# Hybrid trunk kernel: latent norm sums, row maxima and the start of the attention rewritten

## The chip, the core and the metric

The kernel runs on one core of one Trainium2 chip. The metric is the device time of one execution in microseconds (us). The engines are TensorE (PE in the rows; PEld is its weight load), VectorE (DVE), ScalarE (ACT), GpSimd (POOL) and SyncE (SP), which issues every DMA of this kernel in one queue.

## The reference

Two layers work on 768 tokens (256 context, 512 latent) of width 1024. Each layer projects the tokens to three head groups (a state space mixer, latent attention, retention), joins them, projects back and normalizes. Layer 1 returns latent tokens alone. What the change touches is the latent attention:

```python
def rms_norm(x, g):
    xf = x.astype(jnp.float32)
    return (xf * lax.rsqrt(jnp.mean(xf * xf, -1, keepdims=True) + RMS_EPS)).astype(x.dtype) * g

def project(cq, ckv, kr, rope):            # inside mla_mixer
    q = (rms_norm(cq, q_norm) @ w_uq).reshape(b, n, 8, 64 + 32)
    kv = (rms_norm(ckv, kv_norm) @ w_ukv).reshape(b, n, 8, 64 + 64)
    ...                                    # split into nope/rope parts, rope on latent tokens

def mla_attend(q_nope, q_rope, k_nope, k_rope, v):
    s = (jnp.einsum('bqhd,bkhd->bhqk', q_nope, k_nope)
         + jnp.einsum('bqhr,bkr->bhqk', q_rope, k_rope)).astype(jnp.float32) * MLA_SCALE
    pr = jax.nn.softmax(s, axis=-1).astype(v.dtype)
    return jnp.einsum('bhqk,bkhd->bqhd', pr, v)
```

cq is 384 wide, ckv 256 wide. There are 8 heads. Context queries see context keys, latent queries see all.

## The kernel before

All activations lie transposed: a tile is 128 channels by 768 tokens, and the 768 tokens are 6 chunks of 128. A product of full precision is made of three fp32r matmuls (`mm3`): each operand is split into a rounded high part and the remainder (`split`: one ScalarE cast, one VectorE subtraction), and the low-times-low product is left out.

A layer runs in stages: the input projection with the state space mixer, the retention (`ret`), the gate tiles (`zstage`, products `pj`), the preparation of the attention (`mla_prep`), the norm of the mixer (`ztail`), the attention (`mla`), and the output projection in two halves: `out_s` (products `po` with `sh`, `sl`; eight tiles) and `out_m` (`po` with `mr`, `mh`). A scheduler reorders the instructions of each engine by priority and dependence, so the written order sets priorities and not positions: work written later fills places where earlier work is not ready. Each engine then runs its own list strictly in order.

`mla_prep` normalizes ckv and cq (`normed`, L877). For each tile of 128 channels it loads `nx`, makes the scaled high and low parts `nh` and `nl`, squares `nx` on ScalarE and sums the squares over channels with fp32 matmuls against ones into the rows of one PSUM tile (`pn`, L892). `rowcols` (L659) copies those rows to SBUF and turns them with four fp32 matmuls into columns (`pcol`), one column for each chunk; `rstd_all` takes the inverse square root of the columns on VectorE (`rya`) and spreads it back with fp32 matmuls against the identity (`prs`). Then come the key product `pkn`, the value product `pvv` and the query product `pq`, with weights `pwh`, `pwl`.

The attention holds two buffers of operands, one for even and one for odd heads (`mla`, L966). `mla_max` (L985) loads a head's queries, keys and values, splits them, forms the score of the high parts for each chunk of 128 queries (`pmx`), takes the negated row maxima on VectorE (`nm`), splits these into two bf16 tiles (`nmh`, `nml`) and turns each chunk's column into a row with two bf16 matmuls against an identity (`pnm`). ScalarE copies the row to row 96 of the query operand `bqh`, so that the score product (`psc`, 97 rows) subtracts the maximum. `mla_head` (L1022) makes the scores, two exponentials (`pe`, `peh`), a subtraction (`pel`) and the value product (`ppv`). `mla_max` of head h+1 is written ahead of `mla_head` of head h.

`load_mix` (L407) loads the four retention outputs `m` (tile `mraw`) and splits them to `mr`, which `out_m` uses; it is written ahead of the attention.

Of the kernel before, what the change touches and what calls it, by code (L numbers as in the profile page):

```python
# [8 lines left out]

F32 = mybir.dt.float32  # L10
F32R = mybir.dt.float32r
BF16 = mybir.dt.bfloat16
I32 = mybir.dt.int32
AF = mybir.ActivationFunctionType
ALU = mybir.AluOpType
# [16 lines left out]
XP = 776  # L32
XC = 772

(C_ID, C_MF, C_MB, C_R1, C_R2, C_OD, C_PF, C_PB, C_SD, C_SM, C_S2, C_PE, C_PR, NCONST) = (
    0, 128, 256, 384, 512, 640, 768, 896, 1024, 1152, 1280, 1283, 1285, 1287)

(P_CW, P_CB, P_D, P_NW, P_QN, P_KN, P_BA, P_LG, P_LB, P_RF, P_RB, P_DT, P_AL, P_RR, NPC) = (
    0, 60, 72, 80, 88, 91, 93, 117, 125, 133, 135, 137, 169, 201, 209)

RROW = {NCTX: 0, 0: 64}

Z_T, X_T, B_T, Q_T, KV_T, G_T, RQ_T, RK_T, RG_T, RV_T, M_T, NWIN = (
    0, 8, 16, 20, 23, 25, 29, 31, 33, 37, 41, 42)
# [23 lines left out]
def const_pack():  # L68
    p = np.arange(128)
    j, i = p[:, None], p[None, :]  # L70
    c = np.zeros((128, NCONST), np.float32)
    c[:, C_ID:C_ID + 128] = j == i
    c[:, C_MF:C_MF + 128] = j <= i
    c[:, C_MB:C_MB + 128] = j >= i
    c[:, C_R1:C_R1 + 128] = np.maximum(i - j, 0)
    c[:, C_R2:C_R2 + 128] = np.maximum(j - i, 0)
    c[:, C_OD:C_OD + 128] = (1.0 + (j == i)) * 0.125
    c[:, C_PF:C_PF + 128] = i + 1 + 0 * j
    c[:, C_PB:C_PB + 128] = 128 - i + 0 * j
    first = (p % 32 == 0).astype(np.float32)  # L80
    c[:, C_SD:C_SD + 128] = 1.0 / DM
    c[:, C_SM:C_SM + 128] = 1.0 / (DM // 2)
    c[:, C_S2] = first
    c[:, C_S2 + 1] = p % 32 == 1
    c[:, C_S2 + 2] = 0
    c[:, C_PE] = 127 - p
    c[:, C_PE + 1] = p
    c[:, C_PR] = first * (p >= 64)
    c[:, C_PR + 1] = first * (p < 64)
    return c  # L90


class Trunk:
# [146 lines left out]
    def consts(self):  # L240
        nc = self.nc
        c = self.cp.tile([128, 8, 2], F32, name="cT")
        self.load(c, self.A["cT"])
        self.pc = [self.cp.tile([128, NPC], F32, name=f"pc{l}") for l in range(DEPTH)]
        self.load(self.pc[0], self.A["pc"][0])
        self.K = self.cp.tile([128, NCONST], F32, name="K")
        self.load(self.K, self.A["cpack"])
        k = lambda a, n=128: self.K[:, a:a + n]
        self.ident, self.mf, self.mb = k(C_ID), k(C_MF), k(C_MB)
        self.selD, self.selM, self.sel2 = k(C_SD), k(C_SM), k(C_S2, 2)  # L250
        self.ones = self.cp.tile([128, 128], F32, name="ones")
        nc.vector.memset(self.ones, 1.0)
        self.rsb = self.cp.tile([128, T], F32, name="rsb")
        self.identb = self.cp.tile([128, 128], BF16, name="identb")
        nc.vector.tensor_copy(self.identb, self.ident)
        self.mod = [self.cp.tile([128, 24, 2], F32, name=f"mod{l}") for l in range(DEPTH)]
        self.sil = self.cp.tile([128, 8, 32], F32, name="sil")
        nc.vector.memset(self.sil, 0.0)
        v = self.cp.tile([128, 8, 2], F32, name="cv")
        self.ts(v, c, 0.5, ALU.mult)  # L260
        th = self.cp.tile([128, 8, 2], F32, name="cth")
        self.act(th, v, AF.Tanh)
        self.stt(self.sil[:, :, 0:2], th, 1.0, v, ALU.add, ALU.mult)
# [65 lines left out]
    def layer(self, l):  # L329
# [44 lines left out]
        with self.lpool(f"mixr{l}") as MR:  # L374
            self.mr = [[MR.tile([128, T], F32R, name=f"mr{i}{t}") for t in range(4)] for i in range(2)]
            self.m3 = MR.tile([128, T], F32, name="m3")
            self.load_mix(range(4, 8), *self.mr)
            with self.lpool(f"mla{l}") as P, self.ppool(f"mlaps{l}") as self.px:
                self.mla(P)
                for t in range(8):  # L380
                    self.out_s(t)
                with self.tc.high_priority():
                    self.mla_last(P)
            self.mixpool.close()
            if l + 1 < DEPTH:
                self.open_h(l + 1)
            with self.rpool(f"mixm{l}") as R, self.lpool(f"outm{l}") as P, self.ppool(f"outmp{l}") as self.px:
                self.out_m(R, P)
# [267 lines left out]
    def blocks(self):  # L656
        return ([(0, NCTX)] if self.ctx else []) + [(NCTX, T)]

    def rowcols(self, P, prow, bl):  # L659

        rows = P.tile([128, 512], F32, tag="rrow", name="rrow", bufs=1)
        pc = self.ps("prs", "pcol", 1)
        nr = 64 * len(bl)
        if nr == 128:
            self.nc.gpsimd.memset(rows[64:128, NCTX:512], 0.0)
        for a, b in bl[::-1]:
            r = slice(RROW[a], RROW[a] + 64)
            self.copy(rows[r, 0:b - a], prow[r, 0:b - a])
        for c in range(4):
            cs = slice(c * 128, c * 128 + 128)  # L670
            if nr == 128 and c < 2:
                self.mm(pc[:, c:c + 3:2], rows[:, cs], self.K[:, C_PR:C_PR + 2])
            else:
                self.mm(pc[:, c + 2:c + 3], rows[:nr, cs], self.K[:nr, C_PR + 1:C_PR + 2])
        return pc

    def rstd_all(self, P, pc, bl, scale, eps, out):

        c0 = bl[0][0] // 128
# [190 lines left out]
    def mla_prep(self, P):  # L870
# [7 lines left out]
        def normed(src, nt, col, width, full):  # L878
            a0 = 0 if full else NCTX
            hi, lw = [], []  # L880
            bl = ([(0, NCTX)] if full else []) + [(NCTX, T)]
            prow = self.ps("prow", "pn", 1)
            for t in range(nt):
                x = P.tile([128, T], F32, tag="nx", name="nx", bufs=3)
                self.load(x[:, a0:], src[t][:, a0:])
                h = P.tile([128, T], F32R, tag="nhl", name="nh", bufs=6)
                w = P.tile([128, T], F32R, tag="nhl", name="nl", bufs=6)
                self.split(h[:, a0:], w[:, a0:], x[:, a0:], pc[:, col + t:col + t + 1])
                self.act(x[:, a0:], x[:, a0:], AF.Square)
                for a, b in bl:  # L890
                    g = RROW[a] + 32 * (t % 2)
                    self.mm(prow[g:g + 32, 0:b - a], self.ones[:, 0:32], x[:, a:b],  # L892
                            start=t < 2, stop=t >= nt - 2, skip_group_check=True)
                hi.append(h)
                lw.append(w)
            rb = P.tile([128, T], F32, tag="nrb", name="nrb", bufs=1)
            y = self.rstd_all(P, self.rowcols(P, prow, bl), bl, 1.0 / width, RMS_EPS, rb)
            return hi, lw, rb, y

        kh, kl, krb, ky = normed(D["ckv"], 2, P_KN, 256, True)  # L900
# [64 lines left out]

    def mla(self, P):  # L966
        nc, ctx = self.nc, self.ctx
        self.B = []
        for i in range(2):
            b = dict(  # L970
                qh=P.tile([97, T], F32R, name=f"bqh{i}"), ql=P.tile([97, T], F32R, name=f"bql{i}"),
                kh=P.tile([97, T], F32R, name=f"bkh{i}"), kl=P.tile([97, T], F32R, name=f"bkl{i}"),
                vh=P.tile([128, NCH, 128], F32R, name=f"bvh{i}"), vl=P.tile([128, NCH, 64], F32R, name=f"bvl{i}"))
            nc.vector.memset(b["ql"][96:97, :].bitcast(F32), 0.0)
            nc.vector.memset(b["kh"][96:97, :].bitcast(F32), 1.0)
            nc.vector.memset(b["kl"][96:97, :].bitcast(F32), 0.0)
            nc.vector.memset(b["vh"][:, :, 64:128].bitcast(F32), 1.0)
            self.B.append(b)
        self.mla_max(P, 0)
        for h in range(8):  # L980
            if h + 1 < 8:
                self.mla_max(P, h + 1)
            self.mla_head(P, h)

    def mla_max(self, P, h):  # L985

        nc, D, ctx, lo = self.nc, self.D, self.ctx, self.lo
        b, (p, s) = self.B[h % 2], divmod(h, 2)
# [8 lines left out]
        self.split(b["qh"][0:96, lo:], b["ql"][0:96, lo:], q[:, lo:])  # L997
        self.split(b["kh"][0:96, :], b["kl"][0:96, :], k)
        self.split(b["vh"][:, :, 0:64], b["vl"], self.vr[:, :, s * 64:(s + 1) * 64])
        qt = [0, 1, 2, 3, 4, 5] if ctx else [2, 3, 4, 5]  # L1000
        nq = len(qt)
        nm = P.tile([128, 6], F32, tag="nm", name="nm", bufs=2)
        for i, c in enumerate(qt):
            p1 = self.px.tile([128, 1024], F32, tag="pmx", name="pmx", bufs=1)
            n = NCTX if c < 2 else T
            for a in range(0, n, 512):
                self.mm(p1[:, a:min(a + 512, n)], b["qh"][0:96, c * 128:(c + 1) * 128], b["kh"][0:96, a:min(a + 512, n)])
            nc.vector.tensor_reduce(nm[:, i:i + 1], p1[:, 0:n], axis=AX.X, op=ALU.max, negate=True)  # L1008
        nmh = P.tile([128, 6], BF16, tag="nmh", name="nmh", bufs=2)
        nml = P.tile([128, 6], BF16, tag="nml", name="nml", bufs=2)  # L1010
        nc.vector.tensor_copy(nmh[:, 0:nq], nm[:, 0:nq])
        self.tt(nml[:, 0:nq], nm[:, 0:nq], nmh[:, 0:nq], ALU.subtract)
        for a, bnd in self.blocks():
            pr = self.px.tile([128, 1024], F32, tag="pmx", name="pnm", bufs=1)
            for c in range(a // 128, bnd // 128):
                i = qt.index(c)
                o = pr[96:97, c * 128 - a:c * 128 - a + 128]
                self.mm(o, nmh[:, i:i + 1], self.identb, True, False)
                self.mm(o, nml[:, i:i + 1], self.identb, False, True)
            self.copy(b["qh"][96:97, a:bnd], pr[96:97, 0:bnd - a])  # L1020

    def mla_head(self, P, h):  # L1022
        nc, l, D, ctx, lo = self.nc, self.l, self.D, self.ctx, self.lo
# [322 lines left out]
```

## Time and profile before

| | us |
|---|---|
| runs | 1520.98, 1524.68, 1530.27 (median 1524.68) |
| profiled execution, own time | 1519.79 |
| its span | 1518.0 |
| PE busy | 1440.9 (95%) |
| DVE, ACT, POOL busy | 1107.2, 716.9, 46.6 |

The span is the time from the first to the last instruction that the profile shows. A busy share is an average over stages; what limits a stage is seen in the waits inside it. A row of the timeline gives the start and the length of an instruction, and in brackets how long its engine had been idle before it and what ended that idle time. Matmuls overlap: a row's length is longer than the time that it adds, so the price of one is the distance between starts.

### The profile page before, as it was taken

How to read it: one execution, taken by the hardware profiler on the slowest of the kernel's cores; microseconds unless marked ns; L12 is line 12 of the kernel's file. 1: busy time of each engine (PE TensorE's matmuls, PEld its weight loads, DVE VectorE, ACT ScalarE, POOL GpSimd, SP SyncE). 2: the span in 40 equal slices, each digit the busy share in tenths (PEclk: the TensorE clock that was granted, in tenths of full speed). 3: DMA queues.
4: the chain of work that ended last, by engine and by line, in shares of the span. 5: the costliest groups of instructions: out<-in, count | busy, mean ns of one | idle time of the engine just before them, and what ended most of it. 6: DMA issues, size and time to landing. Idle time of an engine off the chain costs nothing. (4 is left out here: it accounts for less than half of the span.)

```text
span 1518.0 us, 24021 instructions
## 1 busy us (share of the span) xinstructions
PE 1440.9 (95%) x8916; PEld 1169.3 (77%) x8916; DVE 1107.2 (73%) x2161; ACT 716.9 (47%) x1420; POOL 46.6 (3%) x45
## 2 busy tenths in 40 slices
PE   7999999999999998999999789999999999989985
PEld 4787789778888776777788668788778877867675
DVE  3599995984574568777545878997786767788767
ACT  2356653662322434477623424565462345257743
POOL 0000000000000000000002230000000000000010
PEclk9999999999999999999999899999999999999998
DMA  8335653657617555434343233353257375653243
GB/s 332 131 111 172 198 164 121 175 178 258 217 62 231 202 157 160 160 122 122 109 149 112 94 123 114 112 144 109 99 180 243 109 227 177 194 164 89 73 149 111
DMA packets 114189, 233.50 MB, mean 154 GB/s; under 512 B 14028, under 2 KB 45644, under 8 KB 113816
## 3 DMA queue, kind: packets, MB, share of 16 engines
q1 hardware_dynamic: 114072, 231.97, 47.5%
q8 instruction: 70, 1.15, 0.3%
q14 instruction: 47, 0.39, 0.1%
HBM read 181.73 MB, written 50.20 MB: 153 GB/s over the span
## 5 line engine op out<-in xcount | busy, mean ns | idle before, releaser
L105 PE MATMUL pj<-hh,wh 128*128 128x512 f32 (+2 forms) x984 | 354.8, 361 | 2.0 <-ACT hh L119 1.6
L105 PE MATMUL pj<-hh,wl 128*128 128x512 f32 (+1 forms) x984 | 353.3, 359 | 0.0
L105 PE MATMUL pj<-hl,wh 128*128 128x512 f32 (+1 forms) x984 | 349.7, 356 | 0.0
L126 ACT CAST wh<-wr 128x1024 fp32r<-128x1024 f32 (+1 forms) x132 | 137.1, 1040 | 232.8 <-PE pj L105 94.1
L105 PEld LDWEIGHTS pj<-hh,wh 128*128 128x128 f32 (+1 forms) x984 | 185.5, 189 | 37.1 <-issue 12.2
L108 DVE TENSOR_TENSOR wl<-wr,wh 128x1024 fp32r<-128x1024 f32 (+1 forms) x132 | 163.5, 1239 | 67.2 <-ACT wh L126 65.0
L105 PEld LDWEIGHTS pj<-hh,wl 128*128 128x128 f32 x984 | 185.3, 188 | 32.7 <-issue 10.6
L105 PEld LDWEIGHTS pj<-hl,wh 128*128 128x128 f32 x984 | 185.7, 189 | 29.4 <-issue 7.3
L111 DVE SCALAR_TENSOR_TENSOR cv<-xpad,cw,cv 128x772 f32<-128x772 f32 (+1 forms) x96 | 92.3, 999 | 0.3
L108 DVE TENSOR_TENSOR pel<-pe,peh 128x512 fp32r<-128x512 f32 (+1 forms) x112 | 71.5, 647 | 25.6 <-ACT peh L119 24.1
L119 ACT ACTIVATE pe<-psc 128x512 f32<-128x512 f32 (+1 forms) x112 | 63.7, 569 | 51.0 <-PE psc L105 47.9
L1008 DVE TENSOR_REDUCE nm<-pmx 128x1 f32<-128x768 f32 (+1 forms) x80 | 67.8, 847 | 15.3 <-PE pmx L105 14.3
L105 PE MATMUL po<-sh,wh 128*128 128x512 f32 (+1 forms) x192 | 70.3, 370 | 2.1 <-DVE oy L111 1.5
L105 PE MATMUL po<-sl,wh 128*128 128x512 f32 (+1 forms) x192 | 69.6, 365 | 0.8 <-DVE sl L111 0.8
L105 PE MATMUL po<-sh,wl 128*128 128x512 f32 (+1 forms) x192 | 69.6, 365 | 0.0
L119 ACT ACTIVATE ce<-cf 64x512 f32<-64x512 f32 (+1 forms) x80 | 47.0, 587 | 45.6 <-DMA cf<-cum 44.6
L119 ACT ACTIVATE tm<-sf,dt 128x128 f32<-128x128 f32 x160 | 53.1, 393 | 30.9 <-DVE sf L108 29.2
L119 ACT ACTIVATE peh<-psc 128x512 fp32r<-128x512 f32 (+1 forms) x112 | 63.5, 567 | 1.0 <-PE ppv L105 0.7
L105 PE MATMUL po<-mr,wh 128*128 128x256 f32 (+1 forms) x256 | 58.8, 316 | 4.0 <-DVE la L111 3.1
L119 ACT ACTIVATE arg<-arg,ncb 128x128 f32<-128x128 f32 x160 | 54.5, 394 | 3.0 <-DVE arg L111 2.6
L105 PE MATMUL pv<-wl,hh 128*128 128x256 f32 x192 | 53.7, 279 | 0.9 <-DVE wl L108 0.9
L105 PE MATMUL pv<-wh,hh 128*128 128x256 f32 x192 | 53.6, 279 | 0.8 <-ACT wh L126 0.8
(333 smaller groups left out, 3062.6 us busy)
## 6 DMA issues: line engine op xcount, KB each, us to landing
wr<-in_win SPq DMA_DIRECT2D x82, 512.0 KB, 3.3
ar<-in_wada SPq DMA_DIRECT2D x48, 512.0 KB, 5.0
wr<-in_wout SPq DMA_DIRECT2D x48, 512.0 KB, 3.4
cf<-cum SPq DMA_DIRECT2D x80, 256.0 KB, 4.2
y<-ys SPq DMA_DIRECT2D x20, 256.0 KB, 2.3
xs<-th SPq DMA_DIRECT2D x16, 256.0 KB, 4.9
x<-in_xT SPq DMA_DIRECT2D x8, 384.0 KB, 9.8
rv<-stv SPq DMA_DIRECT2D x24, 128.0 KB, 4.4
```

The costliest lines, as they stand in the source:

```text
L105: return self.nc.tensor.matmul(out, lhsT=lhsT, rhs=rhs, start=start, stop=stop, **k)
L108: return self.nc.vector.tensor_tensor(out, a, b, op=op)
L111: return self.nc.vector.scalar_tensor_tensor(out, in0=a, scalar=s, in1=b, op0=op0, op1=op1)
L119: return self.nc.scalar.activation(out, in_, f, **k)
L126: self.nc.scalar.copy(hi, raw)
L1008: nc.vector.tensor_reduce(nm[:, i:i + 1], p1[:, 0:n], axis=AX.X, op=ALU.max, negate=True)
```

## The change

Three edits are made, and two consequences of them.

- Latent norms: the squares of the 2 or 3 tiles are added on VectorE, and the sum is taken over channels by one fp32 matmul a chunk (the sum as stationary operand, one column of ones moving), straight into the columns `pcol`. `pn`, the row copies and `rowcols` with its constants are gone.
- Row maxima: `nm` is written as fp32r, and one fp32r matmul a chunk against an fp32r identity takes the place of two bf16 ones. The row lands on partition 0 and is copied to row 96 of `bqh`.
- Attention: `mla_max` is cut into `mla_ops` (loads and splits) and `mla_max`. Head 0's operands are written first, then `out_s` of tiles 0 to 2, then head 0's maxima. `load_mix` moves behind head 0. The 16 memsets of the operand buffers go from VectorE to GpSimd.

```diff
@@ constants, class Trunk @@
-        self.identb = self.cp.tile([128, 128], BF16, name="identb")
-        nc.vector.tensor_copy(self.identb, self.ident)
@@ layer @@
-            self.load_mix(range(4, 8), *self.mr)
             with self.lpool(f"mla{l}") as P, self.ppool(f"mlaps{l}") as self.px:
                 self.mla(P)
-                for t in range(8):
+                for t in range(3, 8):
                     self.out_s(t)
@@ rowcols: removed; normed (in mla_prep) @@
-            prow = self.ps("prow", "pn", 1)
             for t in range(nt):
                 ...
                 self.act(x[:, a0:], x[:, a0:], AF.Square)
-                for a, b in bl:
-                    g = RROW[a] + 32 * (t % 2)
-                    self.mm(prow[g:g + 32, 0:b - a], self.ones[:, 0:32], x[:, a:b],
-                            start=t < 2, stop=t >= nt - 2, skip_group_check=True)
+                if t:
+                    self.tt(sq[:, a0:], sq[:, a0:], x[:, a0:], ALU.add)
+                else:
+                    sq = x
             rb = P.tile([128, T], F32, tag="nrb", name="nrb", bufs=1)
-            y = self.rstd_all(P, self.rowcols(P, prow, bl), bl, 1.0 / width, RMS_EPS, rb)
+            pcol = self.ps("prs", "pcol", 1)
+            for c in range(a0 // 128, NCH):
+                self.mm(pcol[:, c:c + 1], sq[:, c * 128:(c + 1) * 128], self.ones[:, 0:1])
+            y = self.rstd_all(P, pcol, bl, 1.0 / width, RMS_EPS, rb)
@@ mla @@
+        self.identr = P.tile([128, 128], F32R, name="identr")
+        nc.vector.tensor_copy(self.identr, self.ident)
         ...
-            nc.vector.memset(b["ql"][96:97, :].bitcast(F32), 0.0)
+            nc.gpsimd.memset(b["ql"][96:97, :].bitcast(F32), 0.0)
             ...
+        self.mla_ops(P, 0)
+        for t in range(3):
+            self.out_s(t)
         self.mla_max(P, 0)
         for h in range(8):
             if h + 1 < 8:
+                self.mla_ops(P, h + 1)
                 self.mla_max(P, h + 1)
             self.mla_head(P, h)
+            if h == 0:
+                self.load_mix(range(4, 8), *self.mr)
@@ mla_max: loads and splits go to mla_ops, word for word @@
-        nm = P.tile([128, 6], F32, tag="nm", name="nm", bufs=2)
+        nm = P.tile([128, 6], F32R, tag="nm", name="nm", bufs=2)
         ...
-        nmh = P.tile([128, 6], BF16, tag="nmh", name="nmh", bufs=2)
-        nml = P.tile([128, 6], BF16, tag="nml", name="nml", bufs=2)
-        nc.vector.tensor_copy(nmh[:, 0:nq], nm[:, 0:nq])
-        self.tt(nml[:, 0:nq], nm[:, 0:nq], nmh[:, 0:nq], ALU.subtract)
         ...
-                o = pr[96:97, c * 128 - a:c * 128 - a + 128]
-                self.mm(o, nmh[:, i:i + 1], self.identb, True, False)
-                self.mm(o, nml[:, i:i + 1], self.identb, False, True)
-            self.copy(b["qh"][96:97, a:bnd], pr[96:97, 0:bnd - a])
+                self.mm(pr[0:1, c * 128 - a:c * 128 - a + 128], nm[:, i:i + 1], self.identr)
+            self.copy(b["qh"][96:97, a:bnd], pr[0:1, 0:bnd - a])
```

How this moves instructions shows at three places of layer 0. The line numbers of the kernel after differ by a few.

SP's queue where `mla_prep` begins, before (`m` are the retention outputs in memory, `mraw` their copy back, `nx` the latent tiles):

```order
L102 DMA m_0_613<-rgt 128x256
L102 DMA m_0_615<-rgt 128x256
L102 DMA mraw<-m_0_612 128x768
L102 DMA mraw<-m_0_613 128x768
L102 DMA mc<-in_rope 128x512
L102 DMA msn<-in_rope 128x512
L102 DMA nx<-ckv_0_579 128x768
L102 DMA wr<-in_wout 128x1024
L102 DMA g_0_584<-st 128x768
L102 DMA nx<-ckv_0_580 128x768
```

The two `mraw` loads, which need the outputs stored just ahead of them, stand in front of the first `nx`, and a weight load and a gate store stand in front of the second.

The same place in the changed kernel:

```order
L97 DMA m_0_611<-rgt 128x256
L97 DMA m_0_613<-rgt 128x256
L97 DMA ox<-in_xT 128x768
L97 DMA mc<-in_rope 128x512
L97 DMA msn<-in_rope 128x512
L97 DMA nx<-ckv_0_577 128x768
L97 DMA nx<-ckv_0_578 128x768
L97 DMA wr<-in_wout 128x1024
L97 DMA g_0_582<-st 128x768
```

An input load (`ox`, of the first `out_s`) stands where the `mraw` loads were, and both `nx` loads stand together.

TensorE in the norm of ckv, before (the second `pn` and what follows):

```order
L105 MATMUL pj<-hl_7_106,wh 128x256
L105 MATMUL pj<-hh_7_98,wl 128x256
L105 MATMUL pn<-nx,ones 32x256
L105 MATMUL pn<-nx,ones 32x512
L105 MATMUL pkn<-nh,pwh 128x512
L105 MATMUL pkn<-nl,pwh 128x512
L105 MATMUL pkn<-nh,pwh 128x256
L105 MATMUL pkn<-nl,pwh 128x256
L105 MATMUL pcol<-K,rrow 128x2 x2
```

The `pn` pair stands at the end of a gate product, four `pkn` that need only `pwh` follow, then the columns.

The same place in the changed kernel:

```order
L100 MATMUL pj<-hh_6_95,wl 128x256
L100 MATMUL pcol<-ones,nx 128x1 x6
L100 MATMUL pj<-hh_7_96,wh 128x256
L100 MATMUL pj<-hl_7_104,wh 128x256
L100 MATMUL pj<-hh_7_96,wl 128x256
L100 MATMUL pkn<-nh,pwh 128x512
L100 MATMUL pkn<-nl,pwh 128x512
L100 MATMUL pkn<-nh,pwh 128x256
L100 MATMUL pkn<-nl,pwh 128x256
L100 MATMUL pkn<-nh,pwl 128x512
```

One wait place (`pcol`) is left of the two `pn` and the old `pcol`; the `pkn` that need `pwl` now follow at once, where 18 other matmuls stood between before.

TensorE at the first maxima of layer 0, before:

```order
L105 MATMUL po<-sh_5953,wl 128x512
L105 MATMUL po<-sh_5954,wh 128x512
L105 MATMUL po<-sl_5962,wh 128x512
L105 MATMUL po<-sh_5954,wl 128x512
L105 MATMUL pmx<-bkh_6049,bqh_6047 128x256
L105 MATMUL po<-sh_5947,wh 128x256
```

Here 24 `po` stand between the last `prs` of the norm ahead and the first `pmx`.

The same place in the changed kernel:

```order
L100 MATMUL po<-sh_5939,wh 128x256
L100 MATMUL po<-sl_5947,wh 128x256
L100 MATMUL po<-sh_5939,wl 128x256
L100 MATMUL pr<-ar,sil 32x128 x8
L100 MATMUL pmx<-bkh_6020,bqh_6018 128x256
L100 MATMUL po<-sh_5932,wh 128x512
```

Now 96 `po` stand there. Between the first and the last `psc` of layer 0 the number of `po` with `sh` or `sl` falls from 139 to 113.

## Rows read from the trace of the kernel before

**Rows 1.** Page, part 1: busy time, share of the span and instructions of each engine.

```profile
PE 1440.9 (95%) x8916; PEld 1169.3 (77%) x8916; DVE 1107.2 (73%) x2161; ACT 716.9 (47%) x1420; POOL 46.6 (3%) x45
```

**Rows 2.** Windows: length, then each engine's busy time, granted clock, DMA.

```profile
497.70:504.50 6.80, 6.80 (x36) 5.71 (x36) 5.32 (x14) 2.88 (x5) 0.31 (x1) 0.50 0.53 158
...
594.60:600.10 5.50, 0.98 (x4) 0.37 (x3) 3.44 (x6) 3.32 (x5) 0.00 (x0) 1.00 1.00 277
600.10:603.50 3.40, 3.40 (x17) 3.40 (x18) 3.06 (x6) 0.00 (x0) 0.00 (x0) 0.50 0.37 123
621.00:770.00 149.00, 148.49 (x835) 112.24 (x834) 104.94 (x177) 99.45 (x200) 0.00 (x0) 1.00 0.34 108
...
1385.00:1445.00 60.00, 56.12 (x258) 38.24 (x257) 44.71 (x74) 44.44 (x83) 0.00 (x0) 1.00 0.29 89
```

**Rows 3.** Timeline of PE, norm of ckv, layer 0: start, length, idle before.

```profile
491.58 1.05 PE L105 MATMUL pn<-nx,ones 128*32 128x256 f32 x4 [1.17 <-ACT nx L119]
...
496.75 1.05 PE L105 MATMUL pn<-nx,ones 128*32 128x256 f32 x4 [2.03 <-ACT nx L119]
497.73 0.79 PE L105 MATMUL pkn<-nh,pwh 128*128 128x512 f32 x1
...
504.54 0.40 PE L105 MATMUL pkn<-nh,pwl 128*128 128x512 f32 x1
...
508.05 1.06 PE L105 MATMUL prs<-K,rya 128*128 128x128 f32 x8
508.87 0.47 PE L105 MATMUL pj<-hh,wh 128*128 128x512 f32 x1
```

**Rows 4.** Timeline of DVE in the same place.

```profile
501.94 1.21 DVE L108 TENSOR_TENSOR pwl<-pwr,pwh 128x1024 fp32r<-128x1024 f32 x1
```

**Rows 5.** Timeline of SP's queue ahead of it (lengths include waits).

```profile
476.94 5.43 SPq L102 DMA_DIRECT2D mraw<-m  x2
...
483.37 0.43 SPq L102 DMA_DIRECT2D nx<-ckv  x1
```

**Rows 6.** Timeline of PE, and one row of ACT, attention start, layer 0.

```profile
599.00 0.39 PE L105 MATMUL pmx<-bkh,bqh 96*128 96x256 f32 x1 [3.99 <-ACT bkh L126]
599.92 0.43 PE L105 MATMUL po<-sh,wh 128*128 128x256 f32 x1 [0.54 <-DVE oy L111]
...
605.72 0.38 PE L105 MATMUL pr<-K,rows 128*128 128x2 f32 x2 [0.61 <-ACT rows L122]
...
606.94 0.51 PE L105 MATMUL po<-sh,wh 128*128 128x512 f32 x1 [0.62 <-DVE mod L116]
...
597.38 0.83 ACT L126 CAST mr<-mraw 128x768 fp32r<-128x768 f32 x1 [1.32 <-DMA mraw<-m]
```

**Rows 7.** Timeline of PE, layer 1: norm of ckv, then the attention's start.

```profile
1248.85 1.05 PE L105 MATMUL pn<-nx,ones 128*32 128x256 f32 x4 [1.43 <-ACT nx L119]
...
1332.98 0.50 PE L105 MATMUL po<-sh,wh 128*128 128x512 f32 x1 [0.95 <-DVE oy L111]
...
1343.62 0.22 PE L105 MATMUL pnm<-identb,nmh 128*1 128x128 bf16 x1 [1.26 <-DVE nmh L1011]
...
1344.29 0.22 PE L105 MATMUL pnm<-identb,nml 128*1 128x128 bf16 x1 [0.45 <-DVE nml L108]
```

**Rows 8.** Timeline of PE, layer 1: the maxima rows of one later head.

```profile
1380.36 0.22 PE L105 MATMUL pnm<-identb,nml 128*1 128x128 bf16 x1
...
1380.70 0.22 PE L105 MATMUL pnm<-identb,nml 128*1 128x128 bf16 x1
1380.85 0.49 PE L105 MATMUL ppv<-pel,bvh 128*128 128x512 f32 x1
1381.18 0.39 PE L105 MATMUL ppv<-peh,bvh 128*128 128x512 f32 x1
1381.41 0.39 PE L105 MATMUL ppv<-peh,bvl 128*64 128x512 f32 x1
```

**Rows 9.** All instructions on the rows of maxima: lengths in ns, first and last start.

```profile
L105 PE MATMUL pnm<-identb,nmh x80: 217/218/219, 616.6 to 1430.4; 128*1 128x128 bf16 x80
```

More of the change, by code (lines that the diff above doesn't have):

```diff
@@ L11 @@
 F32R = mybir.dt.float32r
-BF16 = mybir.dt.bfloat16
 I32 = mybir.dt.int32
@@ L33 @@
 XC = 772
-(C_ID, C_MF, C_MB, C_R1, C_R2, C_OD, C_PF, C_PB, C_SD, C_SM, C_S2, C_PE, C_PR, NCONST) = (
-    0, 128, 256, 384, 512, 640, 768, 896, 1024, 1152, 1280, 1283, 1285, 1287)
+(C_ID, C_MF, C_MB, C_R1, C_R2, C_OD, C_PF, C_PB, C_SD, C_SM, C_S2, C_PE, NCONST) = (
+    0, 128, 256, 384, 512, 640, 768, 896, 1024, 1152, 1280, 1283, 1285)
 (P_CW, P_CB, P_D, P_NW, P_QN, P_KN, P_BA, P_LG, P_LB, P_RF, P_RB, P_DT, P_AL, P_RR, NPC) = (
     0, 60, 72, 80, 88, 91, 93, 117, 125, 133, 135, 137, 169, 201, 209)
-RROW = {NCTX: 0, 0: 64}
 Z_T, X_T, B_T, Q_T, KV_T, G_T, RQ_T, RK_T, RG_T, RV_T, M_T, NWIN = (
@@ L87, in const_pack @@
     c[:, C_PE + 1] = p
-    c[:, C_PR] = first * (p >= 64)
-    c[:, C_PR + 1] = first * (p < 64)
     return c
@@ L657, in blocks @@
         return ([(0, NCTX)] if self.ctx else []) + [(NCTX, T)]
[L659 to L675, printed above, removed]
     def rstd_all(self, P, pc, bl, scale, eps, out):
@@ L973, in mla @@
                 vh=P.tile([128, NCH, 128], F32R, name=f"bvh{i}"), vl=P.tile([128, NCH, 64], F32R, name=f"bvl{i}"))
-            nc.vector.memset(b["ql"][96:97, :].bitcast(F32), 0.0)
-            nc.vector.memset(b["kh"][96:97, :].bitcast(F32), 1.0)
-            nc.vector.memset(b["kl"][96:97, :].bitcast(F32), 0.0)
-            nc.vector.memset(b["vh"][:, :, 64:128].bitcast(F32), 1.0)
+            nc.gpsimd.memset(b["ql"][96:97, :].bitcast(F32), 0.0)
+            nc.gpsimd.memset(b["kh"][96:97, :].bitcast(F32), 1.0)
+            nc.gpsimd.memset(b["kl"][96:97, :].bitcast(F32), 0.0)
+            nc.gpsimd.memset(b["vh"][:, :, 64:128].bitcast(F32), 1.0)
             self.B.append(b)
+        self.mla_ops(P, 0)
+        for t in range(3):
+            self.out_s(t)
         self.mla_max(P, 0)
@@ L981, in mla, with mla_ops @@
             if h + 1 < 8:
+                self.mla_ops(P, h + 1)
                 self.mla_max(P, h + 1)
             self.mla_head(P, h)
-    def mla_max(self, P, h):
+            if h == 0:
+                self.load_mix(range(4, 8), *self.mr)
+    def mla_ops(self, P, h):
         nc, D, ctx, lo = self.nc, self.D, self.ctx, self.lo
@@ L999, in mla_max @@
         self.split(b["vh"][:, :, 0:64], b["vl"], self.vr[:, :, s * 64:(s + 1) * 64])
+    def mla_max(self, P, h):
+        nc, ctx = self.nc, self.ctx
+        b = self.B[h % 2]
         qt = [0, 1, 2, 3, 4, 5] if ctx else [2, 3, 4, 5]
-        nq = len(qt)
-        nm = P.tile([128, 6], F32, tag="nm", name="nm", bufs=2)
+        nm = P.tile([128, 6], F32R, tag="nm", name="nm", bufs=2)
         for i, c in enumerate(qt):
```

## The prediction

> **What bounds the kernel now.** I read the busy shares first: TensorE is busy for 1440.9 of 1518.0 us [rows 1], so the time is TensorE's work plus its idle time plus what a lowered clock costs. Then the windows, by stage, to see where TensorE is not full. The attention of layer 0 is full: 148.49 of 149.00 us at a granted clock of 1.00 [rows 2]; what is taken off TensorE there is taken off the span, and DVE or ACT work there is covered. Three places are not full. The timeline of the norm of ckv in layer 0 shows TensorE idle for 1.17 and 2.03 us ahead of the two `pn`, waiting for the squares on ScalarE [rows 3]; right behind it the granted clock is 0.50, that is 1.2 in place of 2.4 GHz, for 6.80 us [rows 2]. At the start of the attention of layer 0, TensorE waits 3.99 us for the first head's keys, then 0.54, 0.61 and 0.62 us [rows 6], and another 3.40 us are granted 0.50 [rows 2]. Layer 1 has the same two places, smaller: 1.43 us, and 0.95, 1.26 and 0.45 us [rows 7]. All these places are touched by the change.
>
> **The change, part by part.** The sum is made against the profiled execution's own 1519.8 us.
>
> *Norm matmuls.* There are 10 `pn` groups (five tiles in each layer); one adds 0.98 us (496.75 to 497.73 [rows 3]), so they give back 10 us. The new column sums are fp32 with two passes a matmul, as the old: 6+6+6+4 = 22 matmuls against 16, 12 passes more. A short fp32 pass adds 0.10 us (eight `prs` in 0.82 us [rows 3]), so +1.2. The additions (six on VectorE) take the place of seven row copies on ScalarE; both lie beside TensorE's work except in the chain to `pcol`, which comes next.
>
> *The wait in the norm, layer 0.* Before, idle time of 3.20 us and half of 6.80 us at the lower clock are lost, 6.6 together. SP's queue no longer holds at the two `mraw` (5.43 us [rows 5]), so the first `nx` can be issued some 4 us earlier and the second moves up with it; the sum is then ready about when TensorE comes to `pcol`. But the `pkn` with `pwl` now follow at once. `pwl` began at 501.94 and lasted 1.21 [rows 4], and TensorE used it at 504.54 [rows 3]; its weight load and the VectorE work ahead of it (key rope, a weight split, a gate) hardly move. TensorE will come to it some 4 us earlier than VectorE delivers. So what was lost at `pn` is mostly lost again at `pkn`: I take 1 us of gain. Ends: the whole 6.6 gained, or 3.4 more lost if a second stretch of 6.8 us runs at 0.50.
>
> *The norm in layer 1.* One of the two waits stays, with work ahead of it: −0.5 (ends −1.4 and +1).
>
> *Start of the attention, layer 0.* Idle 5.76 us and half of 3.40 are lost now, 7.5. `mr` on ScalarE stood ahead of the keys' cast and itself waited 1.32 us for its load [rows 6]; it moves behind head 0, and 96 instead of 24 `po` stand ahead of the first `pmx`, some 17 us of work in which the loads land. I take −6.5 and leave 1 us for a weight that comes late (ends −7.5 and 0). *Layer 1:* 2.66 us of waits shown; the bf16 split (`nmh`, `nml`) that causes 1.71 of it is gone: −2.5 with the smaller ones behind (ends −3.5 and 0).
>
> *Row maxima.* 80 pairs of bf16 matmuls [rows 9] become 80 single fp32r ones. In a run, bf16 matmuls start 0.057 us apart (six steps from 1380.36 to 1380.70), and a run costs about 0.19 more: the last is followed after 0.15, and the next matmul takes 0.33 instead of 0.23 [rows 8]. With at least two runs a head (32), 160 × 0.057 + 32 × 0.19 = 15 us go. No row has an fp32r matmul of 128 columns. The lower end is the bf16 spacing, 0.057, with 24 runs of at most 0.19 (half taken): 80 × 0.057 + 2.3 = 7, a change of −8. The upper end is the fp32 row of the same 128 columns and the same identity, two passes, 0.20 each [rows 3]: 16 + 2.3 = 18, a change of +3. I take the upper end: an operand of four bytes and the same shape is the nearest row.
> The Trainium skill ("TensorE: Matmul & The Clock Gate", Back-to-back issue gap) gives the gap of a matmul by its columns alone, 55.8 ns at 128; by it the new matmul would cost what the bf16 one does and the sum would be 11 us lower. The fp32 rows at 0.20 show that columns alone do not decide for every type.
>
> *Moved work.* The 16 memsets leave VectorE for an engine that is 3% busy [rows 1]; the operands' memsets have the 96 `po` as cover, and without it `pmx` would wait for a fraction of a microsecond each. The splits of `mr` (eight casts, eight subtractions) now lie in the attention, where ACT is busy for 99 of 149 us [rows 2]: nothing. Their loads too are moved behind head 0's loads in SP's queue, where `out_m` needs them much later.
>
> Sum: −10 + 1.2 − 1 − 0.5 − 6.5 − 2.5 + 3 = −16.3, so 1503.5 us. The median of the runs shown lies 4.9 us above the profiled execution (0.3%), which I do not add: 1504 us.
>
> **The rivals.**
> 1. *The fp32r matmul of 128 columns flows like the bf16 one.* For it: the weight is one column, and fp32r matmuls elsewhere are single passes. Against: the fp32 row. Its term is −8 in place of +3: 1492.5 us. Chance 0.32. The gap by columns of the Trainium skill ("TensorE: Matmul & The Clock Gate", above) would end here.
> 2. *The fillers are missed.* Layer 0 has 113 instead of 139 `po` between the first and last `psc`. Where layer 1 runs almost without fillers, TensorE is busy for 56.12 of 60.00 us [rows 2], 6.5% idle. If layer 0's 149 us become as thin, 9.7 us are lost, or the same by new waits in the norms and half clocks: 1513 us. Against: 113 are still many, and a place that is full by 99.7% has slack. Chance 0.17.
> 3. *Slower: the maxima do not pipeline.* Each fp32r matmul has a one-column weight of its own; if passes of this form wait for each other, one pass costs its whole length, 0.34 us (eight `prs` last 1.06, seven steps of 0.103 off [rows 3]), and if it takes two, a matmul costs 0.68: 80 × 0.68 + 24 × 0.19 = 59 against 15, that is +44 in place of +3. With the other terms (−19.3) +24.7: 1544 us. It decides from 0.37 us a matmul on. Against: bf16 matmuls of the same shape start 0.057 apart while each lasts 0.22 [rows 8]. Chance 0.05.
>
> **How the numbers follow.** The forecast, 1504 us, has 0.46. A measurement of this kernel can tell about 1%, 15 us, from no change. Of the forecast's 0.46, whose stalls may come out 7 us either way, I count 0.30 as faster and 0.16 as same; rival 1 gives 0.30 and 0.02; rival 2 0.02, 0.14 and 0.01 slower; rival 3 0.05 slower. Together 0.62, 0.32 and 0.06. The range takes in rival 1 with its stalls on the good side (1485) and rival 2 with the runs' median in place of the profiled time (1522).
>
> **What would show it.** In the changed profile: no `pn`, and 44 passes of `pcol` with sums; two starts of neighbouring `pnm` 0.2 us apart (0.057 for rival 1, 0.3 or more for rival 3); TensorE's wait in the ckv norm of layer 0 of 3 to 5 us, ended by `pwl` or `pwh`; no wait over 1 us ahead of the first `pmx` of either layer; the window of layer 0's attention still full. The prediction is wrong if the norm of layer 0 has no wait left (6 us better), if the granted clock falls at new places (3.4 us for each 6.8), or if layer 0's attention shows idle time ended by ScalarE.

## The result and the profile after

| us | before | changed |
|---|---|---|
| median of the runs beside each other | 1527.71 | 1511.14 (1508.57 to 1514.68) |
| profiled execution, own time | 1519.79 | 1511.36 |
| its span, mean granted clock | 1518.0, 0.982 | 1509.5, 0.977 |

The ratio is 0.990, interval 0.9872 to 0.9929. The forecast of 1504 us lies 7 us below the median. The two profiled executions differ by 8.4 us only, mostly because that of before ran at a high clock (0.982; 10 of the 93 runs used below have that or more). To keep clock and work apart, every run is split in two: span times mean granted clock (**time at full clock**, idle time included), and the rest of the span (**lost to the clock**). Over 93 runs of the kernel before, the means are 1490.9 and 33.9; its profiled execution has 1490.7 and 27.3. The five runs of the changed kernel have 1477.1 and 32.0. So the change took 13.8 us at full clock; the 1.9 us from the clock are within the scatter of five runs.

The split has a flaw to keep in mind: where TensorE waits at half clock (1.2 in place of 2.4 GHz), half of the wait is booked as lost to the clock too, though no run shows that the wait would be shorter at full clock. Counted as half of TensorE's busy time at half clock, the loss is, as an estimate, some 19 us in the profiled execution of before (27.3 by the split) and 23 in that of the changed kernel (34.7).

TensorE's busy time fell by 12.9 us against [rows 1]. Part 1 of the page after:

```profile
PE 1428.0 (95%) x8814; PEld 1169.0 (77%) x8814; DVE 1099.7 (73%) x2120; ACT 713.2 (47%) x1413; POOL 55.8 (4%) x58
```

The windows of the places of [rows 2], after:

```profile
496.10:503.90 7.80, 5.36 (x29) 4.01 (x30) 6.03 (x17) 2.74 (x4) 0.00 (x0) 0.56 0.64 216
...
616.50:623.40 6.90, 6.24 (x17) 4.89 (x17) 4.49 (x8) 2.74 (x5) 0.00 (x0) 0.51 0.77 276
625.00:749.00 124.00, 121.46 (x642) 91.00 (x642) 91.35 (x139) 90.22 (x185) 0.00 (x0) 1.00 0.32 100
1310.00:1336.00 26.00, 19.45 (x80) 14.50 (x79) 16.59 (x22) 7.06 (x10) 1.61 (x3) 0.93 0.75 213
1377.00:1437.00 60.00, 55.38 (x247) 38.42 (x246) 45.03 (x66) 45.24 (x86) 0.00 (x0) 1.00 0.30 91
```

The half clock is still there in the norm, and twice as long at the start of the attention of layer 0. The attention of layer 0, full before, is idle for 2.54 us, and at the start of layer 1's TensorE is busy for 19.45 of 26.00 us. The same start before:

```profile
1320.00:1345.00 25.00, 21.60 (x104) 16.85 (x102) 21.09 (x30) 8.17 (x11) 0.00 (x0) 1.00 0.80 233
```

TensorE in the norm of ckv, layer 0, after (answers to [rows 3]):

```profile
491.91 1.50 PE L100 MATMUL pcol<-ones,nx 128*128 128x1 f32 x12
...
496.10 0.50 PE L100 MATMUL pkn<-nh,pwh 128*128 128x512 f32 x1 [2.24 <-ACT pwh L121]
...
499.50 0.79 PE L100 MATMUL pkn<-nh,pwl 128*128 128x512 f32 x1 [2.44 <-DVE pwl L103]
```

No `pn` is left and `pcol` is not waited for. The wait now stands at the key weight: 4.68 us, where the two `pn` had 3.20.

TensorE at the start of the attention, layer 0 (answers to [rows 6]):

```profile
603.19 0.38 PE L100 MATMUL pmx<-bkh,bqh 96*128 96x256 f32 x1
...
614.63 0.28 PE L100 MATMUL pnm<-identr,nm 128*1 128x128 f32 x2 [0.64 <-DVE nm L996]
616.12 0.40 PE L100 MATMUL pnm<-identr,nm 128*1 128x128 f32 x4 [1.21 <-ACT bqh L117]
617.18 0.58 PE L100 MATMUL pmx<-bkh,bqh 96*128 96x256 f32 x1 [0.66 <-ACT bqh L117]
```

ScalarE beside it:

```profile
614.86 0.83 ACT L121 CAST mr<-mraw 128x768 fp32r<-128x768 f32 x1
615.71 0.36 ACT L117 CAST bqh<-pnm 1x256 fp32r<-1x256 f32 x1
```

The first `pmx` waits for nothing (3.99 before), as forecast. But the `po` are used up by the time the last maximum is done, and the chain of maximum, row and row copy stands bare, the copy behind a cast of `mr`.

TensorE in layer 1, norm and attention start (answers to [rows 7]):

```profile
1244.04 0.50 PE L100 MATMUL pkn<-nh,pwl 128*128 128x512 f32 x1 [1.04 <-DVE pwl L103]
...
1320.16 0.79 PE L100 MATMUL po<-sh,wh 128*128 128x512 f32 x1 [4.01 <-DVE oy L106]
...
1326.11 0.61 PE L100 MATMUL pmx<-bkh,bqh 96*128 96x512 f32 x2 [0.91 <-ACT bkh L121]
...
1330.41 0.61 PE L100 MATMUL pmx<-bkh,bqh 96*128 96x512 f32 x2 [1.12 <-DVE nm L996]
...
1331.53 0.50 PE L100 MATMUL po<-sh,wh 128*128 128x512 f32 x1 [0.51 <-DVE oy L106]
```

VectorE ahead of the 4.01 us:

```profile
1317.03 1.23 DVE L103 TENSOR_TENSOR wl<-wr,wh 128x1024 fp32r<-128x1024 f32 x1 [3.85 <-ACT wh L121]
...
1318.63 0.69 DVE L103 TENSOR_TENSOR mr<-mraw,mr 128x512 fp32r<-128x512 f32 x1 [0.24 <-ACT mr L121]
1319.36 0.75 DVE L106 SCALAR_TENSOR_TENSOR oy<-po,mod,rsb 128x512 f32<-128x512 f32 x1
```

`oy`, which frees the accumulator of the last `po`, stands on VectorE behind a weight split that waits for its weight and behind a split of `mr`. The weight's cast on ScalarE had waited 6.02 us, until a `po` of TensorE ended:

```profile
1315.95 1.04 ACT L121 CAST wh<-wr 128x1024 fp32r<-128x1024 f32 x1 [6.02 <-PE po L100]
```

By these rows the chain runs in a ring, from `po` over `wh`, `wl` and `oy` back to `po`.

The row matmuls by form, lengths in ns (answers to [rows 9]):

```profile
L100 PE MATMUL pnm<-identr,nm x80: 218/222/227, 614.6 to 1423.1; 128*1 128x128 f32 x80
```

One run of them in layer 1 (answers to [rows 8]):

```profile
1345.03 0.40 PE L100 MATMUL pnm<-identr,nm 128*1 128x128 f32 x4
1345.27 0.45 PE L100 MATMUL ppv<-pel,bvh 128*128 128x512 f32 x1
```

Four start within 0.24 us: 0.06 each, where the prediction's sum has 0.20.

### The profile page after: what moved, and what is told of

Same layout as the page of the kernel before. It is cut to its first block, busy times and chain, and to the rows that moved or that the text cites. A ratio compares the mean times of both kernels' runs of the same rounds, so it can differ in the third digit from the quotient of the medians.

```text
span 1509.5 us, 23829 instructions
## 1 busy us (share of the span) xinstructions
PE 1428.0 (95%) x8814; PEld 1169.0 (77%) x8814; DVE 1099.7 (73%) x2120; ACT 713.2 (47%) x1413; POOL 55.8 (4%) x58
## 5 line engine op out<-in xcount | busy, mean ns | idle before, releaser
L103 DVE TENSOR_TENSOR wl<-wr,wh 128x1024 fp32r<-128x1024 f32 (+1 forms) x132 | 164.7, 1248 | 67.5 <-ACT wh L121 62.3
L996 DVE TENSOR_REDUCE nm<-pmx 128x1 fp32r<-128x768 f32 (+1 forms) x80 | 67.6, 845 | 16.8 <-PE pmx L100 16.1
```

Source lines behind the costliest of these rows:

```text
L103: return self.nc.vector.tensor_tensor(out, a, b, op=op)
```

## The experiments

**The three edits, alone and in pairs.** Each kernel is the one before with the named edits of the diff ahead, word for word.

```diff
# e1: normed() of the changed kernel, rowcols removed
# e2: nm as fp32r, identr, one matmul a chunk; nmh, nml removed
# e3: mla_ops / out_s(0..2) / mla_max(0), load_mix behind head 0, memsets on gpsimd
# e5 = e1 + e3    e6 = e1 + e2    e9 = e2 + e3
```

e1: 

> The kernel before with the latent norms alone changed (squares added, one fp32 column sum a chunk). Theory A, the terms of the prediction: -10 for the pn groups, +1.2 for the passes, -1.5 for the waits, so about 10 us faster than before (ratio 0.9935), with no pn in the trace, 44 passes of pcol, and in the ckv norm of layer 0 a new TensorE wait of 3 to 5 us ended by pwh or pwl. Rival: the new wait brings lowered clock with it or is longer than what stood at pn, and the edit gives 5 us or less (ratio 0.9965 or more).

e2: 

> The kernel before with the row maxima alone changed (80 fp32r matmuls of 128 columns for 80 bf16 pairs). The prediction took 0.20 us for each: +3, less 1.7 us of waits for the bf16 split in layer 1, so no change (+1, ratio 1.001) and neighbouring pnm 0.2 us apart. The rival, that they flow like bf16: -8 and -1.7, about 10 us faster (ratio 0.9935), and neighbouring pnm 0.06 us apart.

e3: 

> The kernel before with the start of the attention alone changed: operands of head 0 first, three tiles of out_s, then the maxima; load_mix behind head 0; memsets on GpSimd. The prediction: -6.5 in layer 0 and -1 in layer 1 (the rest of its term there belonged to the bf16 split), about 7.5 us faster (ratio 0.995). The rival, read from the changed kernel's trace: the waits only move (in layer 0 to the row copy bqh behind the casts of mr on ScalarE, in layer 1 to oy behind wl and mr on VectorE), so between 3 us faster and 5 us slower (ratio 0.998 to 1.003).

e5: 

> The changed kernel with the bf16 maxima put back (norm and order edits together). If the three edits simply add: 5.0 + (-2.9) faster, about 2 us faster than before (ratio 0.9985). If the fp32r maxima are what makes the order edit pay (the bf16 split lengthens the chain of maxima that the order edit has stripped of its fillers, and the clock falls behind those waits), the lowered clock should cost about 40 us or more as in the order edit alone, against 32 in the changed kernel, the time at full clock about 1477, so 1518 to 1524 us. If the norm edit is what cures the order edit, it is near the changed kernel: 1511 to 1515.

e6: 

> The changed kernel without the order edit. If the edits add: 5 us (norm) and 0.5 us (maxima) faster than before, about 1521 us. If the order edit is worth its -7.2 us at full clock here too, and loses nothing to the clock once the maxima are fp32r, 1518 us (7 us more than the changed kernel). If the order edit brings nothing, near the changed kernel: 1511 to 1513.

e9: 

> The changed kernel without the norm edit (maxima and order edits together). If the edits add, as each stood alone: 3.2 - 1.6, about 1528 us. If the norm edit and the order edit each pay once the maxima are fp32r, it is the changed kernel plus what the norm edit gave given the others; by TensorE's work alone that is 9 to 10 us: 1520 to 1521. If the order edit pays only beside the norm edit (with it -5.5 and -5.3, alone +3.2), near the maxima alone or above: 1524 to 1529, with a lowered clock that costs 40 us or more.

| edits | median us | ratio to before (interval) | at full clock | lost to the clock |
|---|---|---|---|---|
| none (93 runs) | 1526.3 | | 1490.9 | 33.9 |
| norm (e1) | 1523.3 | 0.9967 (0.9944 to 0.9990) | 1483.5 | 36.6 |
| maxima (e2) | 1524.9 | 0.9997 (0.9976 to 1.0018) | 1489.7 | 33.6 |
| order (e3) | 1529.7 | 1.0019 (0.9999 to 1.0039) | 1484.4 | 43.8 |
| norm, maxima (e6) | 1516.4 | 0.9933 (0.9909 to 0.9956) | 1477.0 | 37.5 |
| norm, order (e5) | 1517.8 | 0.9946 (0.9923 to 0.9969) | 1481.2 | 34.7 |
| maxima, order (e9) | 1524.4 | 0.9984 (0.9965 to 1.0004) | 1481.9 | 40.5 |
| all three | 1511.1 | 0.9900 (0.9872 to 0.9929) | 1477.1 | 32.0 |

The medians do not add: alone the edits give −3.0, −1.4 and +3.4, together −15.2. At full clock −7.4, −1.2 and −6.5 make −15.1, together −13.8, but that nearness is chance, for the pairs do not add: norm and maxima give −13.9 where −8.6 would be the sum, norm and order −9.7 for −13.9, maxima and order −9.0 for −7.7 (the standard error of a mean is at most 0.9 us). What an edit is worth depends on what stands beside it. The clock moves too: +2.7, −0.3 and +9.9 alone, −1.9 together. In this table the order edit loses 40 us or more to the clock where the norm edit is missing, and 32 to 35 beside it; e7 below has both and loses 42.1. That the fp32r maxima make it pay fell with e5, which keeps the bf16 pairs and loses 34.7. The windows of e3 behind its two attention starts:

```profile
634.20:644.40 10.20, 8.36 (x30) 6.10 (x30) 6.67 (x11) 3.95 (x7) 0.00 (x0) 0.50 0.81 267
...
1340.70:1354.40 13.70, 8.78 (x25) 4.91 (x24) 9.01 (x14) 2.65 (x5) 0.00 (x0) 0.50 0.70 209
```

and TensorE at the second:

```profile
1340.34 0.69 PE L105 MATMUL pmx<-bkh,bqh 96*128 96x512 f32 x2 [3.18 <-ACT bkh L126]
1343.34 1.01 PE L105 MATMUL pmx<-bkh,bqh 96*128 96x512 f32 x2 [2.31 <-DVE nm L1018]
1345.40 1.01 PE L105 MATMUL pmx<-bkh,bqh 96*128 96x512 f32 x2 [1.05 <-DVE nm L1018]
1347.46 1.01 PE L105 MATMUL pmx<-bkh,bqh 96*128 96x512 f32 x2 [1.05 <-DVE nm L1018]
```

With 2.06 us from one pair of `pmx` to the next, half of it waiting for the maximum, TensorE stands half idle and 13.7 us run at 1.2 GHz. How many `po` with `sh` or `sl` the scheduler put between the first `pmx` and the first `psc` of layer 1 goes with it: 12 in e3 and 9 in e9, both with a stretch of 13.7 us; 33 in e5 and 29 in the changed kernel, with 3.4 us; 23 to 25 in the four kernels without the order edit, with 0 to 3.4 us. e7 below, with the norm edit, has none and again 13.7 us, so the norm edit as such is not the cure. e8 below has 29 like the changed kernel and 10.2 us, so the number is not all of it. No run changed it alone: that it is the cause is argued, not shown.

**The price of the row matmul.** e8 is the changed kernel with

```diff
-        self.identr = P.tile([128, 128], F32R, name="identr")
-        nc.vector.tensor_copy(self.identr, self.ident)
         ...
-        nm = P.tile([128, 6], F32R, tag="nm", name="nm", bufs=2)
+        nm = P.tile([128, 6], F32, tag="nm", name="nm", bufs=2)
         ...
-                self.mm(pr[0:1, ...], nm[:, i:i + 1], self.identr)
+                self.mm(pr[0:1, ...], nm[:, i:i + 1], self.ident)
```

> The changed kernel with the maxima and the identity in fp32 in place of fp32r: the same 80 matmuls of 128 columns, in the type of the row from which the prediction took its price. If fp32 is what made that row 0.20 us, neighbouring pnm start about 0.2 us apart, the runs cost 80 x 0.14 = 11 us more of TensorE work, and the time is 8 to 11 us longer than the changed kernel (1519 to 1522 us). If the shape sets the price, pnm stay 0.06 us apart and the time is that of the changed kernel.

Measured: 1522.3 us (ratio 0.9978, 0.9958 to 0.9998), 11.2 more than the changed kernel; 1486.5 at full clock, 9.4 more. The row matmuls of e8 by form:

```profile
L100 PE MATMUL pnm<-K,nm x160: 270/272/273, 614.4 to 1431.6; 128*1 128x128 f32 x160
```

One run of them in TensorE's timeline:

```profile
1350.95 1.03 PE L100 MATMUL pnm<-K,nm 128*1 128x128 f32 x8
1351.91 0.50 PE L100 MATMUL ppv<-pel,bvh 128*128 128x512 f32 x1
```

Two passes a matmul, 0.12 us each: 0.24 against 0.06. Shapes and values are those of the changed kernel; the type alone makes the price. 80 × 0.18 are 14.4 us of TensorE's work, more than the time grew by, so part of it presumably fell where TensorE would have waited.

**Fixes of the waits that are left.** (`pslot` loads a weight and splits it.)

```diff
# e4: the changed kernel
-            if h == 0:
+            if h == 4:
                 self.load_mix(range(4, 8), *self.mr)
# e7: the changed kernel; pslot of the key weight one step earlier
+        wk = self.pslot(P, self.A["wukv"][l, 0], 1024)
         kh, kl, krb, ky = normed(D["ckv"], 2, P_KN, 256, True)
# e10: out_s ahead in layer 0 alone
-        for t in range(3):
+        for t in range(3 if ctx else 0):
             self.out_s(t)
# e11: e10 with 2 in place of 3
# e12: e10; krt, rope and kro (VectorE) written behind both pslot of wukv
```

e4: 

> The changed kernel with load_mix behind head 4 in place of head 0. If the loads and splits of mr are what holds the row copy (layer 0) and oy (layer 1), the TensorE waits ahead of the first pnm and of the first score in layer 0 (0.64, 1.21 and 0.66 us, with 6.8 us at half clock behind) and part of the 4.01 us in layer 1 go: 4 to 8 us faster than the changed kernel, so about 21 to 25 us faster than before (ratio 0.984 to 0.986). If the waits come from the order of the heads and the weights themselves, it is the same as the changed kernel (ratio 0.990).

e7: 

> The changed kernel with the load and split of the key weight moved ahead of the norm of ckv. If the two waits of 2.24 and 2.44 us in layer 0, ended by pwh and pwl, and the half clock of 6.8 us behind them are its cost, they go: 4.7 us and up to 3.4 us less, with 1.0 us in layer 1, so 1502 to 1507 us. Rival: the wait moves on to the squares or to rya, and it is within 2 us of the changed kernel (1509 to 1513).

e10: 

> The changed kernel with the three tiles of out_s ahead of the maxima in layer 0 alone; in layer 1 all of them are written behind the heads again. In layer 1 the changed kernel idles for 4.01, 0.91, 1.12 and 0.51 us at this place and has 3.4 us at half clock; the kernel with norm and maxima edits alone idles there for 1.16, 1.04, 1.38 and 0.66 us. If these waits are the price of the order edit in layer 1: 2 to 4 us faster than the changed kernel, 1507 to 1509 us. Rival: the waits come back at other places, and it is 1510 to 1514.

e11: 

> As the run before, with two tiles of out_s ahead of the maxima in layer 0 in place of three. If the chain of the last maximum, the row and its copy (0.64, 1.21 and 0.66 us with 6.8 us at half clock behind) stands bare because the fillers were used up ahead of it, 24 or 48 matmuls more behind it cover it: 3 to 5 us faster than the run before. If the third tile is needed as cover of the loads ahead of the first score of the maxima, a wait of 1 to 4 us comes back there and the time is the same or up to 3 us longer.

e12: 

> The kernel with out_s ahead in layer 0 alone (1510.9 us), and with the rotation of the shared key written behind the load and split of the key and value weights, so that pwl stands ahead of five VectorE instructions of some 3 us. If TensorE's waits for pwl (2.1 us in layer 0, 3.9 in layer 1, each with half clock behind it) are VectorE's order, they shorten by 2 to 3 us each and the time is 1503 to 1508 us. Rival: pwh, its load or the norm's columns take over as what TensorE waits for, and it is 1509 to 1513.

| | median us | ratio to before (interval) | at full clock | lost to the clock |
|---|---|---|---|---|
| changed kernel | 1511.1 | 0.9900 (0.9872 to 0.9929) | 1477.1 | 32.0 |
| e4, load_mix later | 1513.2 | 0.9914 (0.9884 to 0.9944) | 1477.4 | 34.1 |
| e7, key weight earlier | 1517.8 | 0.9943 (0.9916 to 0.9970) | 1474.8 | 42.1 |
| e10, layer 0 alone | 1510.9 | 0.9908 (0.9882 to 0.9935) | 1474.6 | 35.2 |
| e11, two tiles ahead | 1515.3 | 0.9910 (0.9875 to 0.9946) | 1475.8 | 36.3 |
| e12, key rotation later | 1515.6 | 0.9939 (0.9914 to 0.9963) | 1474.3 | 39.4 |

None beats the changed kernel, and e7, e11 and e12 lie above both of the outcomes that were stated for them. e7, e10, e11 and e12 are 1 to 3 us shorter at full clock, at the edge of what so few runs can tell, and give it back, or more, to the clock. e4 moved nothing: the scheduler still drew a cast of `mr` between the two row copies, so its time does not tell whether `mr` is to blame. In e11 the wait for the row copy was longer (2.76 us) than in the changed kernel (1.21): the two tiles' `po` too were used up ahead of it. What held the copy there shows on ScalarE:

```profile
609.66 0.83 ACT L121 CAST mr<-mraw 128x768 fp32r<-128x768 f32 x1 [1.79 <-DMA mraw<-m]
610.52 0.36 ACT L117 CAST bqh<-pnm 1x256 fp32r<-1x256 f32 x1
```

The copy stood behind a cast of `mr` that waited for its load. In e7 such a cast waited 3.08 us, a cast of `wh` followed, and TensorE waited 3.07 us for the copy. So in these two runs it is `mr`, with its load, that holds the copy in the main; no run keeps it behind the copies.

TensorE of e7 in layer 1, where no `po` lie between the `pmx`:

```profile
1334.90 1.01 PE L100 MATMUL pmx<-bkh,bqh 96*128 96x512 f32 x2 [2.37 <-DVE nm L996]
1336.96 1.01 PE L100 MATMUL pmx<-bkh,bqh 96*128 96x512 f32 x2 [1.05 <-DVE nm L996]
1339.02 1.01 PE L100 MATMUL pmx<-bkh,bqh 96*128 96x512 f32 x2 [1.05 <-DVE nm L996]
```

It is the picture of e3, with 13.7 us at half clock. In e10 the 4.01 us ahead of layer 1's attention are gone, and the norm of layer 1 waits longer:

```profile
1240.12 0.50 PE L100 MATMUL pkn<-nh,pwh 128*128 128x512 f32 x1 [1.57 <-ACT pwh L121]
...
1246.61 0.79 PE L100 MATMUL pkn<-nh,pwl 128*128 128x512 f32 x1 [3.92 <-DVE pwl L103]
```

e12 took away most of the waits for `pwl` (1.65 us left of 5.9 in e10), and others stood in their place. TensorE of e12 in the norm of layer 0:

```profile
496.61 0.50 PE L100 MATMUL pkn<-nh,pwl 128*128 128x512 f32 x1 [1.65 <-DVE pwl L103]
501.15 2.05 PE L100 MATMUL prs<-K,rya 128*128 128x128 f32 x8 [1.98 <-DVE rya L106]
```

and in that of layer 1:

```profile
1248.95 0.79 PE L100 MATMUL po<-sh,wh 128*128 128x512 f32 x1 [2.12 <-DVE zt L106]
...
1252.64 0.79 PE L100 MATMUL po<-sl,wh 128*128 128x512 f32 x1 [2.89 <-DVE sl L106]
```

VectorE is busy for 10.22 of the 10.50 us from 1248 on. It seems to have more to deliver there than TensorE's other work covers, so that order only decides which of its results TensorE waits for. That is read from the profiles; no run tests it.

## Why the prediction was right, and where it was not

The direction and the size came out, but two terms were wrong by about 11 us each, in opposite directions. That they cancelled is luck. Profile against profile (8.4 us):

| term | forecast | measured | from |
|---|---|---|---|
| `pn` | −10 | −10 | none left |
| `pcol` | +1.2 | +0.7 | 44 passes; from first start to the next matmul 4.9 in place of 4.2 |
| norm, layer 0 | −1 | +0.3 | waits 4.68, before 3.20; half clock costs 2.2, before 3.4 |
| norm and key products, layer 1 | −0.5 | +2 | waits 1.04, 1.37, 0.37, 1.61; before 1.43, 0.44, 0.44 |
| attention start, layer 0 | −6.5 | −1.5 | waits 2.83, before 5.76; half clock costs 3.1, before 1.7 |
| attention start, layer 1 | −2.5 | +4 | waits 6.55, before 4.05; 3.4 us at half clock are new |
| row maxima | +3 | about −8 | worked out, not measured: 80 × 0.06 and what a run adds, as in rival 1 |
| waits inside the attentions | 0 | +3.6 | 2.65 and 6.00 us idle from the first `psc` to the last `ppv`, before 0.51 and 4.52 |

These make −8.9; the profiles differ by 8.4. (What half clock costs is half of TensorE's busy time in the stretch: `po` of 512 columns start 0.43 us apart in it, 0.23 at full clock.) The nearness flatters the table: by the same rule, half clock at places that the change does not touch cost some 2.4 us more in the second profile, so the sum is about 2 us short of the gain.

- **Norm matmuls, and the wait in the norm of layer 0: right.** The wait moved to `pwh` and `pwl` and is 4.68 us, inside the 3 to 5 forecast. Alone, though, the edit gives 3.0 us where 10 were expected: e1 waits 3.94 us for `pwh` and 1.26 and 3.24 us in layer 1, and loses 2.7 us more to the clock. Beside the other edits it gives more (8.5 beside the maxima, 13.3 beside both).
- **Row maxima: the mis-sized step.** "An operand of four bytes and the same shape is the nearest row" failed. The fp32 row is 0.20 because fp32 takes two passes; fp32r takes one, and flows like bf16 at the same columns (0.06 against 0.057). Rival 1 had the price right, and its time of 1492.5 wrong, since the other terms did not come. Nor did all of the 8 us reach the time: at full clock the maxima edit is worth 1.2 us alone, 2.5 beside the order, 6.5 beside the norm and 4.1 beside both. The Trainium skill ("TensorE: Matmul & The Clock Gate", Back-to-back issue gap) gives 55.8 ns for a matmul of 128 columns taken alone, and about 81 ns in a stream of weight loads and matmuls. The 0.06 of the run above agrees with the first, though each of its matmuls has a weight load of one column (0.08 us long). That formula was a better guide here than a row of another type. For fp32 it doesn't hold: the passes of e8 start 0.12 us apart.
- **Start of the attention: the step that failed.** The forecast counted the waits that go (and the 3.99 us did go), and asked only whether a weight comes late. It did not ask what stands behind the cover: in layer 0 the fillers (the `po` in between) are gone when the maxima need them, in layer 1 `oy` queues on VectorE behind `wl` and `mr`. Of −9 forecast in both layers +2.5 came. e6 against the changed kernel says the same over many runs: at full clock the order edit adds nothing to the other two (1477.0 and 1477.1). What it gives there, 5.3 us, it gives by the clock (37.5 and 32.0).
- **Moved work at 0: nearly right.** Layer 0's attention is 98.0% full (121.46 of 124.00) with 113 `po` in it, so rival 2 came in part, 2 us of its 9.7. A row matmul less also leaves a wait: e2 has the same cheap `pnm` and gains 1.2 us at full clock of the 8 that it takes off TensorE by the sum; its attention of layer 0 idles for 3.13 of 127.00 us, that of before for 0.51 of 149.00. Its time is the "no change" that the prediction's price gave, for another reason.
- **The signs.** The wait in the norm and the 44 passes came. "No wait over 1 us ahead of the first `pmx`" failed in layer 1 (4.01). Of the three signs of being wrong two came: half clock at a new place (3.4 us from 1320, besides 6.8 for 3.4 at the start of layer 0's attention) and idle time in layer 0's attention that ScalarE ended (0.6 us for `bqh`, 0.5 for `den`). The number held all the same.
- **The range.** Its upper end, 1522, does not come out of its terms: 1513 and 4.9 make 1518. The measured time lies inside either.
- **Against a median.** Taking the profiled execution as the base was safe for work and not for the clock: it lost 27.3 us to it where the mean is 33.9. The 4.9 us that the prediction left out would have made 1508, 3 us from the median.

## What to carry to other kernels

Price an instruction from a row of its own type, not only its own shape: the fp32 row was three times too dear for fp32r. When work is moved ahead to cover a wait, count what is left to cover the next one, and which instruction queues behind the moved one on the slower engine. Split each run into time at full clock and time lost to the clock before comparing edits, and run the pairs too: here neither the medians nor the times at full clock added.

## What the runs showed of the hardware

- The granted clock fell to 1.2 GHz without a wait over 1.21 us: in the changed kernel 6.8 us from 616.5 on come with waits of 0.64, 1.21 and 0.66 us with matmuls between them, TensorE being idle for 2.51 of the 3.19 us up to 617.18.
- A matmul of 128 columns with a one-column weight adds 0.057 us in bf16 and 0.06 in fp32r; in fp32 it takes two passes of 0.12, 0.24 in all (e8).
- The time lost to the clock differs from run to run of one kernel, from 24 to 41 us in the first 30 runs of the kernel before, and moves by 10 us between kernels whose time at full clock differs by 2 to 7 (e7 against the changed kernel, e3 against before).
